# Down operands of a feed-forward loaded three units ahead, and a sample fold done by transposes

## The chip, the core and the metric

One core of a Trainium2 chip runs the whole kernel in one launch. The metric is the device time of that launch in microseconds (us); lower is better. A core has TensorE (in the profile PE for its matmuls and PEld for its weight loads), VectorE (DVE), ScalarE (ACT), GpSimd (POOL) and SyncE (SP), which here issues the DMAs. Each engine runs its own queue in order.

## The reference

One layer of a hybrid decoder on 2048 prompt tokens and 64 sample tokens of width 1024. The two sub-layers are a mixer (sliding-window attention beside gated linear attention) and a feed-forward network. The change lies in the second, whose core is:

```python
h = rms_norm(x, g_ffn_pre)
u = jax.nn.relu(jnp.einsum('btd,df->btf', h, w_up))      # w_up (1024, 4096)
f = jnp.einsum('btf,fd->btd', u * u, w_down)             # w_down (4096, 1024)
x = x + rms_norm(f, g_ffn_post)
```

All of it is in float32, for prompt and sample alike.

## The kernel before

Float32 precision is made of three passes: each operand is split into a rounded high part (a ScalarE copy) and the rest (a VectorE subtraction), and a product is high x high, high x low and low x high (`three`, `split_copy`). For the prompt the feed-forward uses a scheme with seven products in place of eight for a 2x2 blocking, so there are sums of blocks before and after the products.

The prompt tokens are worked in two halves (`sb` 0 and 1). For each half `up(sb, fc, ...)` runs over 16 strips of 256 hidden features: seven products of 12 matmuls in the order `UP_ORDER`, with sums and squares behind each (`taken`), and at the end a store of the strip's seven operand blocks to the DRAM tensor `s_d` (1792 KB). Numbers 0, 8 and 9 in the order are the sample tokens, in the first half only: 0 and 8 are their product with the strip's weights, into the bank `sam` (rows are token parts high and low, 128 of them), and `both` is its copy in SBUF. Step 9 turns it to features x tokens and adds the high and low rows, with a matmul against the constant `fold` (two identities on top of one another). `sample_features` squares, splits and stores the result to `sm_d`.

`down(sb)` then walks 112 units: seven products `p` in `DOWN_ORDER`, each over the 16 strips. A unit needs an operand `s` (from `s_d`) and an operand `t` (from `w_down`, or from sums of its blocks kept in `t_d`). `down_operand` loads each into a raw tile (tag `r`, the profile's `rs` and `rt`) and splits it into `o0` and `o1`. Unit n multiplies four 128-column slices, 12 matmuls of 128x512, into the banks `dn`. The next unit's operands are fetched at the head of a unit. The raw tiles have two buffers (three for `s` in the second half), the split ones three. For p in 1, 2, 3 and 5 of the first half two more matmuls take the sample tokens (`dsam`), whose features lie in two tiles `smp` of 512 KB, loaded by `load_sample`.

Beside the units runs a list of work, `todo`, of which some goes out behind each unit: `gather` adds banks into the result rows, `finish` loads the residual rows (`x1`, in the profile `fx`), normalizes and stores a result, `load_h` splits the second half's inputs that `fetch_h` loaded at the units in `H_FETCH`. `prepare_last` and `finish_last` do the last four row tiles. `gains_post` loads the gains of the last norm (`gfpost`).

The order on an engine is set in two ways. Calls through `te`, `ac` and `dv` (class `InOrder`) keep the program's order among themselves. Everything else, the DMAs on SyncE among it, is placed by a scheduler at compile time: it takes what is ready, in the order of the program where several are. A tile of a pool with `bufs=n` can be written again when its reader n tiles back is done. `tc.issue_after(ins)` asks for what is traced within it to be queued behind `ins`.

Of the kernel before, what the change touches and what calls it, by code (L numbers as in the profile page):

```python
# [115 lines left out]
def f32(ap):  # L116
    return ap.bitcast(F32)
# [23 lines left out]
def hybrid_step_kernel(ctx: ExitStack, tc: tile.TileContext, I, O):  # L141
# [1447 lines left out]
    def squared(t, src=None):  # L1589
        ac.activation(t, t if src is None else src, AF.Relu)  # L1590
        ac.activation(t, t, AF.Square)

    def up(sb, fc, before, steps=iter(())):
# [28 lines left out]
        def taken(p):  # L1622

            if p == 1:
                ac.activation(s(1), X, AF.Copy)
            elif p == 5:
                ac.activation(s(3), Z, AF.Copy)
            elif p == 7:
                add(3, s(3), V)
            elif p == 6:  # L1630
                add(1, s(1), Y)
                add(3, s(3), s(1))
                squared(s(3))
# [12 lines left out]

# [121 lines left out]
    def sample_features(fc, sam):  # L1768
        sq = U["sam"].tile([P, 2, NS], F32, tag="samq", name=f"samq_{fc}", bufs=1)
        parts = U["sam"].tile([P, 2, 2 * NS], F32R, tag="samp", name=f"samp_{fc}", bufs=1)  # L1770
        squared(sq, sam[:, FC : FC + 2 * NS].rearrange("p (u t) -> p u t", u=2))
        split_by(ac, dv, parts[:, :, :NS], parts[:, :, NS:], sq)
        nc.sync.dma_start(sm_d[:, fc], f32(parts))

    def down_operand(sb, p, fc, which):

        name, kind = f"{'st'[which]}_{sb}_{p}_{fc}", "st"[which]
        raw = Dp[kind + "r"].tile([P, BT], F32, tag="r", name=f"r{name}", bufs=3 if (sb, which) == (1, 0) else 2)
        hi, lo = (Dp[kind + "s"].tile([P, BT], F32R, tag=f"o{u}", name=f"o{u}{name}", bufs=3) for u in range(2))
# [7 lines left out]
        nc.sync.dma_start(raw, src)  # L1787
        split_copy(hi, lo, raw)
        return hi, lo

# [15 lines left out]
    def finish(i, fi):  # L1806

        n = rows(i)
        x1 = Dp["x1"].tile([P, D], F32, tag="x1", name=f"fx1_{i}", bufs=1)
        nc.sync.dma_start(x1[:n], x1_d[i])  # L1810
# [9 lines left out]
        nc.sync.dma_start(y_rows(i), fi[:n])  # L1820
        yield 1.3
# [3 lines left out]
    def prepare_last(i, j, fi):  # L1825

        x1 = Dp["lx"].tile([P, D], F32, tag=f"lx{j}", name=f"lx1_{i}", bufs=1)
        nc.sync.dma_start(x1, x1_d[i])
# [19 lines left out]
    smp = {}  # L1848

    def load_sample(u, part):  # L1850

        n = NFC // 2
        smp[part] = Dp["smp"].tile([P, n, 2 * NS], F32R, tag=f"smp{part}", name=f"smp_{u}_{part}", bufs=1)
        nc.sync.dma_start(f32(smp[part]), sm_d[:, part * n : (part + 1) * n, u])

    def gather(sb, p, j, f, p_):

# [60 lines left out]
    def down(sb):  # L1918
# [1 line left out]


        units = [(p, fc) for p in DOWN_ORDER for fc in range(NFC)]
        parts, f, todo, late = {}, {}, deque(), DOWN_ORDER[-1]
        fetched, loaded = (dict(zip(units_, H_ORDER)) for units_ in (H_FETCH, [(p, fc + 4) for p, fc in H_FETCH]))

        def fetch(n):
            if n < len(units) and n not in parts:
                parts[n] = [down_operand(sb, *units[n], which) for which in range(2)]

        def products(n, j):  # L1930
            p, fc = units[n]
# [1 line left out]
            q = slice(j * P, (j + 1) * P)  # L1933
            return three(banks[j], sh[:, q], sl[:, q], th, tl, fc == 0, fc == NFC - 1, te)

        fetch(0)
        for n, (p, fc) in enumerate(units):
            if fc == 0:
                banks = [down_bank(f"dn_{sb}_{p}_{j}") for j in range(4)]
# [14 lines left out]
            if (sb, p, fc) == (0, late, 0):  # L1954
# [3 lines left out]
                weights = ahead_of_up()  # L1958
                next(weights)
                todo.extend((*waiting, weights))  # L1960
            fetch(n + 1)
            for j in range(4):
                done = products(n, j)
            if sam is not None:
                for u, t in enumerate(parts[n][1]):
                    te.matmul(
                        sam, smp[fc // 8][:, fc % 8], t, start=fc + u == 0, stop=fc == NFC - 1 and u == 1
                    )
# [38 lines left out]
    fold = cpool.tile([P, NS], F32, name="fold")  # L2007
    nc.vector.tensor_tensor(fold, ident[:, :NS], ident[:, NS:], op=ALU.add)
    last_rows = residual(*early.pop(0), te, ac, dv)
    sums_13(0, 0, dv)  # L2010
    run(load_h(0, 5, ac, dv))
# [76 lines left out]
```

## Time and profile before

| what | value |
|---|---|
| median of 3 runs | 2264.04 us (2259.86 to 2265.18) |
| the profiled execution | 2263.19 us |
| its span, first to last instruction | 2261.4 us |
| mean granted TensorE clock | 0.995 |
| strips of `up`, first half | about 940 to 1283 us |
| units of `down`, first half | 1283 to 1633 us |
| units of `down`, second half | 1941 us to the end |

In a timeline row stand the start, the busy time, the engine, the line of the code, the operation, what is written and read with its shape, how many were merged, and in brackets how long the engine was idle before and who ended that. In a list of waits the three numbers are the total in us, the count and the longest. In a row of the windows stand the busy times of PE, PEld, DVE, ACT and POOL with their counts, then the granted clock, the DMA engines' busy share and GB/s. Matmuls overlap: the time from start to start counts, not the busy time of one.

### The profile page before, as it was taken

To read this page: it belongs to the slowest core of one execution; us is meant where nothing else is said; L and a number is where in the kernel's file an instruction comes from. 1 tells how busy PE (TensorE), PEld (TensorE's weight loads), DVE (VectorE), ACT (ScalarE), POOL (GpSimd) and SP (SyncE) were. 2 spreads that over 40 slices of the span, in tenths; PEclk is the share of its full clock that TensorE was granted. 3 is DMA by queue.
4 is the path that set the end of the run, shared out by engine and by line. 5 is a ranking of instruction groups with operands and counts; after the bars stand their busy time and mean duration, and the time that the engine had idled before them with its cause. 6 is when DMAs were issued, how large, how long until landed. Compare 5 with 4: busy or idle time off the path is not lost.

```text
span 2261.4 us, 34140 instructions
## 1 busy us (share of the span) xinstructions
PE 2183.5 (97%) x11816; PEld 1868.7 (83%) x11816; DVE 1529.9 (68%) x3102; ACT 1221.4 (54%) x2594; POOL 259.4 (11%) x417
## 2 busy tenths in 40 slices
PE   8999999999999999999999999999999999999998
PEld 7888888999998887788888788887888888788876
DVE  5888877776765565777788664447676666455566
ACT  5778766556664444555545564334544454454444
POOL 3566422111111110000000000000000000000000
PEclk9999999999999999999999999999999999999999
DMA  6334322214335558967777885557644443766675
GB/s 231 119 133 143 102 90 82 67 57 148 126 122 196 184 181 312 313 222 243 251 254 253 284 290 181 180 167 231 195 179 154 154 154 140 252 201 198 192 241 169
DMA packets 237256, 417.81 MB, mean 185 GB/s; under 512 B 25172, under 2 KB 137276, under 8 KB 232972
## 3 DMA queue, kind: packets, MB, share of 16 engines
q1 hardware_dynamic: 237084, 415.64, 54.8%
q8 instruction: 93, 1.52, 0.3%
q14 instruction: 79, 0.65, 0.1%
HBM read 268.44 MB, written 148.18 MB: 184 GB/s over the span
## 4 chain that ended last, share of the span: by engine, by line
PE 64%; DVE 15%; ACT 8%; DMA 8%; issue 3%; POOL 1%; SPq 0%; DVEq 0%; ACTq 0%; POOLq 0%
PE dn L130 21%; PE uc L130 6%; PE ua L130 6%; PE out L1250 6%; PE gproj L130 5%; PE ud L130 3%; PE ue L130 3%; PE ub L130 3%; DMA rt<-t_d 3%; DVE s L130 2%; PE proj L130 2%; PE dsam L130 1%; DVE pl L130 1%; PE o L130 1%; PE sam L130 1%
## 5 line engine op out<-in xcount | busy, mean ns | idle before, releaser
L130 PE MATMUL dn<-o0t,o0s 128*128 128x512 f32 x896 | 350.7, 391 | 9.0 <-ACT o0t L218 8.8
L130 PE MATMUL dn<-o1t,o0s 128*128 128x512 f32 x896 | 351.3, 392 | 3.1 <-DVE o1t L219 3.1
L130 PE MATMUL dn<-o0t,o1s 128*128 128x512 f32 x896 | 349.9, 391 | 0.0
L219 DVE TENSOR_TENSOR o1s<-rs,o0s 128x512 fp32r<-128x512 f32 x224 | 154.6, 691 | 197.2 <-ACT o0s L218 182.8
L218 ACT ACTIVATE o0s<-rs 128x512 fp32r<-128x512 f32 x224 | 141.1, 630 | 249.9 <-PE dn L130 206.0
L130 PE MATMUL gproj<-wg,gx 128*128 128x384 f32 x1408 | 268.5, 343 | 0.1
L130 PEld LDWEIGHTS gproj<-wg,gx 128*128 128x128 f32 x1408 | 241.6, 189 | 4.5 <-issue 4.3
L130 ACT ACTIVATE st<-st 128x512 f32<-128x512 f32 x224 | 141.1, 630 | 158.9 <-DVE st L130 154.9
L130 PEld LDWEIGHTS dn<-o0t,o0s 128*128 128x128 f32 x896 | 168.6, 188 | 48.9 <-ACT o0t L218 11.9
L130 PEld LDWEIGHTS dn<-o1t,o0s 128*128 128x128 f32 x896 | 168.5, 188 | 43.7 <-DVE o1t L219 7.9
L130 PEld LDWEIGHTS dn<-o0t,o1s 128*128 128x128 f32 x896 | 168.5, 188 | 35.0
L219 DVE TENSOR_TENSOR o1t<-rt,o0t 128x512 fp32r<-128x512 f32 x224 | 153.9, 687 | 64.3 <-ACT o0t L218 63.9
L218 ACT ACTIVATE o0t<-rt 128x512 fp32r<-128x512 f32 x224 | 139.6, 624 | 91.7 <-DMA rt<-t_d 70.0
L130 PE MATMUL uc<-H,s 128*128 128x512 f32 x768 | 186.7, 391 | 0.0
L130 PE MATMUL ua<-H,w 128*128 128x512 f32 x744 | 179.2, 390 | 0.0
L130 PEld LDWEIGHTS uc<-H,s 128*128 128x128 f32 x768 | 144.1, 188 | 31.9
L130 PEld LDWEIGHTS ua<-H,w 128*128 128x128 f32 x744 | 138.7, 188 | 28.2
L1250 PE MATMUL out<-wo,mt 128*128 128x512 f32 x680 | 158.9, 392 | 1.9 <-ACT mt L218 1.8
L1250 PEld LDWEIGHTS out<-wo,mt 128*128 128x128 f32 x680 | 126.5, 188 | 28.6 <-ACT mt L218 2.1
L208 POOL TENSOR_TENSOR frs<-rs_v,half 128x1 f32<-128x1 f32 (+1 forms) x13 | 8.4, 657 | 1230.2 <-DVE rs_v L206 1230.2
L130 DVE TENSOR_TENSOR st<-st 128x512 f32<-128x512 f32 x160 | 110.7, 692 | 35.1 <-ACT st L130 31.8
L130 ACT ACTIVATE s<-t 128x1024 fp32r<-128x1024 f32 x62 | 65.8, 1061 | 93.5 <-PE ud L130 29.0
(388 smaller groups left out, 4231.2 us busy)
## 6 DMA issues: line engine op xcount, KB each, us to landing
s_d<-st SPq DMA_DIRECT2D x32, 1792.0 KB, 7.6
rs<-s_d SPq DMA_DIRECT2D x224, 256.0 KB, 2.9
raw<-in_w_up SPq DMA_DIRECT2D x64, 512.0 KB, 5.2
rt<-t_d SPq DMA_DIRECT2D x128, 256.0 KB, 3.3
rt<-in_w_down SPq DMA_DIRECT2D x96, 256.0 KB, 2.8
t<-in_w_down SPq DMA_DIRECT2D x64, 256.0 KB, 3.7
t_d<-t SPq DMA_DIRECT2D x32, 512.0 KB, 6.6
gx<-xt_d SPq DMA_DIRECT2D x28, 512.0 KB, 4.8
```

What stands on the lines that cost most here:

```text
L130: ins = call(*a, **k)
L208: nc.gpsimd.tensor_tensor(out, v[:n], e, op=ALU.pow)
L218: nc.scalar.activation(hi, src, AF.Copy)
L219: vector.tensor_tensor(lo, src, f32(hi), op=ALU.subtract)
L1250: te.matmul(banks[c], x, w[:, c * 512 : (c + 1) * 512], start=k + u == 0, stop=k == KT - 1 and u == len(products) - 1,)
```

## The change

- `UP_ORDER`: the sample's second product (8) comes before product 3 in place of behind it.
- Step 9 is two transposes of 128x128 through the identity. `sample_features` adds the two halves itself, with a ScalarE copy and a VectorE add, before the squares.
- `down_operand` is cut in two: `down_raw` loads, three units ahead, into three raw buffers (four in the second half); the split is called two units ahead.
- The sample features are loaded by unit, 64 KB each, into four buffers (`load_sample`).
- `H_FETCH` is moved: its first fetch goes from unit (6, 0) to (6, 6), the one at (6, 8) goes, and one at (3, 8) comes. The gains are called behind unit 26 in place of 8. The loads of `x1` stand in an issue-after clause on the latest unit's last matmul.

```diff
-UP_ORDER, UP_FIRST = (1, 5, 7, 0, 6, 3, 8, 2, 9, 4), (1, 0, 2, 8, 5, 7, 9, 6, 3, 4)
+UP_ORDER, UP_FIRST = (1, 5, 7, 0, 6, 8, 3, 2, 9, 4), (1, 0, 2, 8, 5, 7, 9, 6, 3, 4)
-H_FETCH = ((6, 0), (6, 8), (1, 0), (1, 8), (5, 0), (5, 8), (3, 0))
+H_FETCH = ((6, 6), (1, 0), (1, 8), (5, 0), (5, 8), (3, 0), (3, 8))
...
                 for u in range(2):
-                    te.matmul(
-                        sam[:, FC + u * NS : FC + (u + 1) * NS], both[0][:, u * P : (u + 1) * P], fold, start=True, stop=True
-                    )
+                    te.transpose(sam[:, FC + u * P : FC + (u + 1) * P], both[0][:, u * P : (u + 1) * P], ident)
...
-        squared(sq, sam[:, FC : FC + 2 * NS].rearrange("p (u t) -> p u t", u=2))
+        turned = sam[:, FC:].rearrange("p (u a t) -> p u a t", u=2, a=2)
+        ac.activation(sq, turned[:, :, 1], AF.Copy)
+        dv.tensor_tensor(sq, sq, turned[:, :, 0], op=ALU.add)
+        squared(sq)
...
-    def down_operand(sb, p, fc, which):
+    def down_raw(sb, p, fc, which):
...
-        raw = Dp[kind + "r"].tile([P, BT], F32, tag="r", name=f"r{name}", bufs=3 if (sb, which) == (1, 0) else 2)
-        hi, lo = (Dp[kind + "s"].tile([P, BT], F32R, tag=f"o{u}", name=f"o{u}{name}", bufs=3) for u in range(2))
+        raw = Dp[kind + "r"].tile([P, BT], F32, tag="r", name=f"r{name}", bufs=4 if sb else 3)
...
         nc.sync.dma_start(raw, src)
+        return raw
+
+    def down_operand(sb, p, fc, which, raw):
+
+        name, kind = f"{'st'[which]}_{sb}_{p}_{fc}", "st"[which]
+        hi, lo = (Dp[kind + "s"].tile([P, BT], F32R, tag=f"o{u}", name=f"o{u}{name}", bufs=3) for u in range(2))
         split_copy(hi, lo, raw)
...
-        nc.sync.dma_start(x1[:n], x1_d[i])
+        with tc.issue_after(latest[0].ins):
+            nc.sync.dma_start(x1[:n], x1_d[i])
...
-    def load_sample(u, part):
-
-        n = NFC // 2
-        smp[part] = Dp["smp"].tile([P, n, 2 * NS], F32R, tag=f"smp{part}", name=f"smp_{u}_{part}", bufs=1)
-        nc.sync.dma_start(f32(smp[part]), sm_d[:, part * n : (part + 1) * n, u])
+    def load_sample(p, fc):
+
+        t = Dp["smp"].tile([P, 2 * NS], F32R, tag="smp", name=f"smp_{p}_{fc}", bufs=4)
+        nc.sync.dma_start(f32(t), sm_d[:, fc, int(p in (2, 3))])
+        return t
...
+        def load(n):
+            if n < len(units) and n not in raws_:
+                raws_[n] = [down_raw(sb, *units[n], which) for which in range(2)]
+                if sb == 0 and units[n][0] in (1, 2, 3, 5):
+                    smp[n] = load_sample(*units[n])
+
         def fetch(n):
             if n < len(units) and n not in parts:
-                parts[n] = [down_operand(sb, *units[n], which) for which in range(2)]
+                load(n)
+                parts[n] = [down_operand(sb, *units[n], which, raws_[n][which]) for which in range(2)]
...
+        for n in range(3):
+            load(n)
         fetch(0)
+        fetch(1)
...
-            fetch(n + 1)
+            load(n + 3)
+            fetch(n + 2)
             for j in range(4):
                 done = products(n, j)
+            latest[:] = [done]
...
-            if n == 8:
+            if n == 26:
                 with tc.issue_after(done.ins):
-                    for part in range(2 * (sb == 0)):
-                        load_sample(0, part)
                     gains_post(sb)
-            if p == 5 and sb == 0 and fc in (8, NFC - 1):
-                load_sample(1, fc // 9)
```

More of the change, by code (lines that the diff above doesn't have):

```diff
@@ L1827, in prepare_last @@
         x1 = Dp["lx"].tile([P, D], F32, tag=f"lx{j}", name=f"lx1_{i}", bufs=1)
-        nc.sync.dma_start(x1, x1_d[i])
+        with tc.issue_after(latest[0].ins):
+            nc.sync.dma_start(x1, x1_d[i])
         ssq = Dp["n"].tile([P, 4], F32, tag="lssq", name=f"lssq_{i}", bufs=4)
@@ L1846, in finish_last @@
             nc.sync.dma_start(y_rows(i)[:, dd], fg[:, dd])
[L1848 to L1854 removed]
+    latest = []
+    def load_sample(p, fc):
+        t = Dp["smp"].tile([P, 2 * NS], F32R, tag="smp", name=f"smp_{p}_{fc}", bufs=4)
+        nc.sync.dma_start(f32(t), sm_d[:, fc, int(p in (2, 3))])
+        return t
     def gather(sb, p, j, f, p_):
@@ L1922, in down @@
         units = [(p, fc) for p in DOWN_ORDER for fc in range(NFC)]
-        parts, f, todo, late = {}, {}, deque(), DOWN_ORDER[-1]
+        parts, raws_, smp, f, todo, late = {}, {}, {}, {}, deque(), DOWN_ORDER[-1]
         fetched, loaded = (dict(zip(units_, H_ORDER)) for units_ in (H_FETCH, [(p, fc + 4) for p, fc in H_FETCH]))
+        def load(n):
[3 more added lines that the diff above has]
+                    smp[n] = load_sample(*units[n])
         def fetch(n):
             if n < len(units) and n not in parts:
-                parts[n] = [down_operand(sb, *units[n], which) for which in range(2)]
+                load(n)
+                parts[n] = [down_operand(sb, *units[n], which, raws_[n][which]) for which in range(2)]
         def products(n, j):
@@ L1966, in down @@
                     te.matmul(
-                        sam, smp[fc // 8][:, fc % 8], t, start=fc + u == 0, stop=fc == NFC - 1 and u == 1
+                        sam, smp[n], t, start=fc + u == 0, stop=fc == NFC - 1 and u == 1
                     )
             del parts[n]
-            if n == 8:
+            if n == 26:
                 with tc.issue_after(done.ins):
-                    for part in range(2 * (sb == 0)):
-                        load_sample(0, part)
                     gains_post(sb)
-            if p == 5 and sb == 0 and fc in (8, NFC - 1):
-                load_sample(1, fc // 9)
             if sb == 0 and (p, fc) in loaded:
@@ L2006, in hybrid_step_kernel @@
     down_halves = ((fc, half) for fc in range(NFC) for half in range(2))
-    fold = cpool.tile([P, NS], F32, name="fold")
-    nc.vector.tensor_tensor(fold, ident[:, :NS], ident[:, NS:], op=ALU.add)
     last_rows = residual(*early.pop(0), te, ac, dv)
```

## The prediction

> **What bounds the kernel now.** I read the page's head first, then the list of waits for the whole span, then the same list for single stretches, and last the timelines around the waits.
>
> ```profile
> span 2261.4 us, 34140 instructions
> PE 2183.5 (97%) x11816; PEld 1868.7 (83%) x11816; DVE 1529.9 (68%) x3102; ACT 1221.4 (54%) x2594; POOL 259.4 (11%) x417
> ...
> s_d<-st SPq DMA_DIRECT2D x32, 1792.0 KB, 7.6
> rs<-s_d SPq DMA_DIRECT2D x224, 256.0 KB, 2.9
> ```
>
> TensorE is busy for 97% of the span, and the change leaves the number of down products as it is. So only TensorE's own holes and its few small instructions can be won. The list of waits of TensorE names the holes that the change can reach (columns: total us, times, longest):
>
> ```profile
> PE dn L130 <- ACT o0t L218: 8.8, 7, 3.4
> PE sam L130 <- ACT both L130: 3.2, 4, 1.4
> PE dn L130 <- DVE o1t L219: 3.1, 9, 1.3
> ```
>
> The same list over three stretches: 1545 to 1645 (first two rows), 1950 to 2050 (next two), 2050 to the end (last two):
>
> ```profile
> PE dn L130 <- ACT o0t L218: 2.7, 3, 1.4
> PE dn L130 <- DVE o1t L219: 2.0, 4, 1.3
> ...
> PE dn L130 <- ACT o0t L218: 1.5, 1, 1.5
> PE dn L130 <- DVE o1t L219: 0.4, 2, 0.2
> ...
> PE dn L130 <- ACT o0t L218: 1.1, 2, 0.9
> PE dn L130 <- DVE o1t L219: 0.7, 3, 0.2
> ```
>
> These, with one hole of 3.4 us at 1297, are nearly all the waits of the down products. What a hole costs beyond its idle time is in TensorE's timeline:
>
> ```profile
> 1293.73 0.39 PE L130 MATMUL dn<-o1t,o0s 128*128 128x512 f32 x1
> ...
> 1296.68 0.39 PE L130 MATMUL dn<-o0t,o1s 128*128 128x512 f32 x1
> 1300.44 0.80 PE L130 MATMUL dn<-o0t,o0s 128*128 128x512 f32 x1 [3.37 <-ACT o0t L218]
> ...
> 1303.90 0.40 PE L130 MATMUL dn<-o1t,o0s 128*128 128x512 f32 x1
> ```
>
> From 1293.73 to 1296.68 lie 13 steps, so one product takes 0.227 us from start to start, and a unit of 12 takes 2.72 us. From 1296.68 to 1303.90 lie 8 steps, which took 7.22 us in place of 1.82: this hole cost 5.4 us, of which some 1.9 are the slow products behind it. The windows show the granted clock dip there, and a second stretch with as many products missing at full clock:
>
> ```profile
> 1280.00:1340.00 60.00, 56.41 (x241) 45.31 (x240) 36.09 (x51) 34.49 (x55) 0.00 (x0) 0.97 0.89 292
> 1460.00:1520.00 60.00, 60.00 (x263) 49.09 (x262) 26.43 (x43) 21.57 (x38) 0.00 (x0) 1.00 0.51 166
> 1520.00:1580.00 60.00, 55.98 (x240) 44.37 (x238) 40.59 (x59) 28.22 (x48) 3.35 (x5) 1.00 0.70 227
> ```
>
> The Trainium skill, page "TensorE: Matmul & The Clock Gate", section "What's actually happening", says that one wholly idle window of about 3.4 us puts the array on half its clock; the 3.37 us of idleness and the clock of 0.97 agree, and by that rule a hole that is only shortened already loses its slow products.
>
> **Why the operands were late.** SyncE's queue and ScalarE around the hole at 1297:
>
> ```profile
> 1283.29 0.43 SPq L1854 DMA_DIRECT2D smp<-sm_d  x1
> ...
> 1288.79 0.42 SPq L200 DMA_DIRECT2D gfpost<-in_g_ffn_post  x1
> 1291.07 0.32 SPq L1710 DMA_DIRECT2D s_d<-st  x1
> 1291.43 0.43 SPq L1787 DMA_DIRECT2D rs<-s_d  x1
> ...
> 1299.24 0.63 ACT L218 ACTIVATE o0s<-rs 128x512 fp32r<-128x512 f32 x1 [7.76 <-DMA rs<-s_d]
> ```
>
> The 1.8 MB store of the last strip went out just ahead of the operand load for unit 5, with half-megabyte loads of samples and gains ahead of both, so a load that takes 2.9 us in the median took nearly 8. Two raw buffers let the load of unit n+2 start only when unit n is split. The rows also show that the place in the program does not set the place in the queue. The gains stand in the code behind the products of unit 8, under an issue-after clause on a matmul; they were issued at 1288.79, while unit 5 began at 1300.44. Loads go out as soon as a buffer is free.
>
> **Part by part.**
>
> *Fold by transposes.* TensorE's timeline at the last fold, and at a run of eight transposes of the same 128x128 shape:
>
> ```profile
> 1279.90 0.55 PE L130 MATMUL sam<-fold,both 128*128 128x64 f32 x4
> 1280.26 3.00 PE L130 MATMUL ue<-H,w 128*128 128x512 f32 x12
> ...
> 761.12 1.06 PE L1436 MATMUL xnT<-ident,x 128*128 128x128 f32 x8 [1.10 <-DVE x L1426]
> 761.93 2.33 PE L1250 MATMUL out<-wo,mt 128*128 128x512 f32 x9
> ```
>
> A fold takes 0.36 us of TensorE, eight transposes 0.81, so two take 0.20. Over 16 strips that is 16 x 0.16 = 2.6 us. Between 0 (transposes as dear as the fold) and 2.6 I take 2.6, the measured shape.
>
> *Sample product moved ahead of product 3.* The copy `both` gets a further product (12 steps, 2.72 us) before TensorE asks for it. The longest of its waits is 1.4 us, so all 3.2 us go. The first strip keeps its own order, so a few tenths could stay.
>
> *More work behind the fold.* Each strip gains one ScalarE copy and one VectorE add, and ScalarE must then wait for that add:
>
> ```profile
> 1020.76 0.26 ACT L130 ACTIVATE samq<-sam 128x128 f32<-128x128 f32 x1
> ...
> 1022.57 1.07 ACT L130 ACTIVATE w<-raw 128x1024 fp32r<-128x1024 f32 x1 [0.86 <-PE ue L130]
> ...
> 1028.25 0.60 ACT L130 ACTIVATE st<-uc 128x512 f32<-128x512 f32 x1 [2.13 <-PE uc L130]
> ...
> 1020.89 2.15 DVE L130 TENSOR_TENSOR st<-st 128x512 f32<-128x512 f32 x3 [0.88 <-ACT st L130]
> 1022.95 0.29 DVE L130 TENSOR_TENSOR samp<-samq,samp 128x128 fp32r<-128x128 f32 x1
> ```
>
> The add comes behind VectorE's three, at 1022.95. ScalarE's three remaining sample steps (0.31 each, one size above the 0.26) then end near 1024.2, so the split queued behind them starts 1.6 us late. ScalarE idles 2.13 us before 1028.25, which takes that up before TensorE asks for anything: that split feeds a product four products later. I take 0; uncovered it is 1.6 per strip.
>
> *Raw operands three units ahead, three buffers (four in the second half).* At 1297, one more buffer lets the load of unit 5 go out when unit 2 is split, before the store at 1291.07. The whole 5.4 us go; unit 7, behind the store, still has two units in hand. In the stretch from 1557 another thing holds SyncE:
>
> ```profile
> 1557.90 0.34 SPq L1820 DMA_DIRECT2D out_y_prompt<-f  x1
> 1558.29 0.42 SPq L1810 DMA_DIRECT2D fx<-x_d  x1
> 1559.69 0.32 SPq L1787 DMA_DIRECT2D rs<-s_d  x1
> ...
> 1561.50 0.32 SPq L1787 DMA_DIRECT2D rt<-t_d  x1
> 1565.02 0.34 SPq L1820 DMA_DIRECT2D out_y_prompt<-f  x1
> ```
>
> Each result store stands at the head of the queue until its add is done; two units of loads go out per cycle of 7.1 us, where TensorE wants two per 5.4. A deeper buffer does not mend the cycle, it lends one unit once: of the 4.7 us of waits (2.7 + 2.0) I take 2.72. Bounds: 0, and 23 missing products x 0.227 = 5.2. In the second half the waits are 1.9 (1.5 + 0.4) and 1.8 (1.1 + 0.7), each far below the lead won; I take all 3.7.
>
> *Splits two units ahead in the program.* Still three split buffers, so TensorE frees them as before. 0; the gathers queued behind them get no later than the products they wait for.
>
> *Fetches moved.* The seven H fetches (two loads each on SyncE, with two ScalarE copies of the 1.07 shape and two VectorE subtractions) and the gains (one load) go to later units, the x loads get an issue-after clause on a matmul. As the gains' row shows, none of this need move them in the queue; 0, covered by ScalarE and VectorE, which are busy 21.57 and 26.43 of 60 us in the quiet stretch. Four sample loads of 512 KB become 64 small ones, one SyncE issue of 0.43 each, at most, in 64 units of 14 x 0.227 = 3.18 us; the half megabyte at 1283.29 leaves the crowded start. 0 on the path.
>
> Sum: 2.6 + 3.2 + 5.4 + 2.7 + 3.7 = 17.6. The profiled execution took 2263.19 us (span 2261.4), the median of the runs is 0.85 above it. 2263.2 - 17.6 + 0.85 = 2246.4 us.
>
> **Rivals.**
>
> *The DMA engines are the limit, not the lead.* For it: their busy share of 0.89 at 292 GB/s in 1280 to 1340; loads asked for earlier would merely queue earlier. Against it: 0.51 and 0.70 elsewhere. Only the fold's 5.8 stay: 2258.2, within the bound of 0.3% (6.8 us), which is about what a measurement can tell here.
>
> *The edits of place do nothing.* The gains' row speaks for that; it is in my sum at 0 and changes no number.
>
> *ScalarE's new wait reaches TensorE, slower.* At the end of each strip the in-order chain of ScalarE stands still behind VectorE's add. It decides if TensorE needs something behind that split within the strip. Price 16 x 1.6 = 25.6: 2246.4 + 25.6 = 2272.0. Against it speak the 2.13 us of idleness.
>
> *The small sample loads hold the operand loads, slower.* A sample buffer is freed only by TensorE; a load waiting for it blocks SyncE. If no unit stayed in hand, a unit would take a landing and two ScalarE copies, 2.9 + 2 x 0.63 = 4.2 against 3.18: 64 x 1.0, 2310. It needs both the three units of lead and the four buffers to be gone. The Trainium skill, page "DMA: Bandwidth & Descriptors", section "Rules for kernel authors", says to coalesce many small transfers into large ones, and these are 64 KB each where the old ones are 512; no run here yet shows such a load.
>
> **How the numbers follow.** Forecast 0.75, DMA limit 0.13, ScalarE's wait 0.08, sample loads 0.04. So faster by over 0.3% 0.75, within 0.13, slower 0.12. The low end takes the 1557 stretch at 5.2 instead of 2.7 (2243.9) and the 4 us by which the fastest run lies under the median: 2240. The high end reaches to the DMA case at 2258.2: 2259.
>
> **What would show it.** Right: no wait of `sam` for `both`; two matmul records per strip for the turn where the fold has four; no hole of TensorE near 1297 and a clock of 1.00 there; ScalarE's waits for raw operands gone at the start of both down stages; some waits left after the first results of the first half. Wrong: the same holes with the loads issued earlier but landing no sooner (DMA limit), new waits of `ua` or `ub` for ScalarE's splits, or SyncE waiting for TensorE at the sample loads with ScalarE waiting for operands behind it.

## The result and the profile after

The changed kernel takes 2241.72 us (median of four runs, 2239.81 to 2243.32), the kernel before 2262.93 (four runs, 2259.86 to 2265.18). The ratio is 0.991 with a 95% interval of 0.9898 to 0.9921: 21.2 us faster, where 17.6 were forecast (2246.4). The time lies within the forecast range, near its low end. Three of the five terms that lead to it were off: most of one was lost to a wait that the forecast had at nothing, and two came out larger.

The head of the page of after, and TensorE's waits in the whole span for `dn` and `sam` (total us, times, longest):

```profile
span 2239.4 us, 34249 instructions
PE 2173.6 (97%) x11784; PEld 1865.2 (83%) x11784; DVE 1531.7 (68%) x3117; ACT 1217.7 (54%) x2610; POOL 261.3 (12%) x417
...
PE dn L130 <- DVE samq L130: 2.0, 1, 2.0
PE dn L130 <- DVE o1t L219: 0.7, 3, 0.3
PE dn L130 <- ACT o0t L218: 0.6, 1, 0.6
PE sam L130 <- ACT both L130: 0.5, 1, 0.5
```

The waits for operand splits fell from 11.9 us in 16 places to 1.3 in four, the one for `both` from 3.2 to 0.5. One wait is new: `dn` for `samq`, 2.0 us, once.

Why the operands are now in time is seen best from ScalarE. Its waits in 1275 to 1345, before (first two rows) and after (next three), and in 1945 to 2000, before (one row) and after (one):

```profile
ACT o0s L218 <- DMA rs<-s_d: 11.4, 5, 7.8
ACT o0t L218 <- DMA rt<-t_d: 6.9, 7, 2.1
...
ACT o0s L218 <- PE dn L130: 14.2, 11, 1.7
ACT H L1495 <- DMA hraw<-h_d: 14.1, 7, 3.0
ACT o0t L218 <- DMA rt<-t_d: 0.2, 1, 0.2
...
ACT o0t L218 <- DMA rt<-t_d: 22.6, 11, 5.2
...
ACT o0s L218 <- PE dn L130: 29.2, 19, 1.6
```

Before, the splits waited for loads. After, they wait for TensorE to free a split buffer, which is how a pipeline looks that is far enough ahead. One wait for loads grew, that of the copies of H: 14.1 us, where before had 6.4. It matters below. The operand loads themselves became no quicker: the page gives these medians from issue to landing (last column, us), where before had 7.6 and 2.9:

```profile
s_d<-st SPq DMA_DIRECT2D x32, 1792.0 KB, 8.7
rs<-s_d SPq DMA_DIRECT2D x224, 256.0 KB, 3.5
```

To place the gain I split both spans at the starts of TensorE's stages, taken from its timeline: the up stage, then the seven down products of each half (192 `dn` matmuls each; one without a hole and without the sample products that products 2 to 5 of the first half carry takes 43.5 us). Products are counted by their place in `DOWN_ORDER`: product 6 is the one numbered 7, which some of the expectations below call the seventh product. The up stage is counted from its first sample product, 2.9 us behind its first product. All in us:

| stage | before | after | gain |
|---|---|---|---|
| ahead of the feed-forward | 928.84 | 926.68 | 2.17 |
| up stage of the first half | 354.25 | 347.60 | 6.65 |
| down, first half, product 1 | 49.24 | 47.35 | 1.89 |
| products 2 to 5 | 206.64 | 207.06 | -0.42 |
| product 6 | 50.28 | 44.94 | 5.34 |
| up stage of the second half | 307.79 | 307.79 | 0.00 |
| down, second half, product 1 | 46.53 | 43.52 | 3.01 |
| product 6 | 46.60 | 43.52 | 3.08 |
| the rest (products 7, products 2 to 5 of the second half, the end) | 271.23 | 270.96 | 0.27 |

The first row belongs to no edit: in the executions that follow, this part ends anywhere between 926.0 and 931.5 us. So a single span carries some 2.5 us either way, and below I read the stages first.

### The profile page after: what moved, and what is told of

The parts are those of the page before. It is cut to its first block, busy times and chain, and to the rows that moved or that the text cites. A ratio compares the mean times of both kernels' runs of the same rounds, so it can differ in the third digit from the quotient of the medians.

```text
span 2239.4 us, 34249 instructions
## 1 busy us (share of the span) xinstructions
PE 2173.6 (97%) x11784; PEld 1865.2 (83%) x11784; DVE 1531.7 (68%) x3117; ACT 1217.7 (54%) x2610; POOL 261.3 (12%) x417
## 4 chain that ended last, share of the span: by engine, by line
PE 73%; DVE 13%; ACT 7%; DMA 4%; issue 2%; POOL 1%; SPq 0%; DVEq 0%; ACTq 0%; POOLq 0%
PE dn L130 26%; PE ua L130 7%; PE uc L130 7%; PE gproj L130 6%; PE out L1250 6%; PE ud L130 4%; PE ue L130 4%; PE ub L130 4%; DVE s L130 2%; PE proj L130 2%; PE dsam L130 1%; PE sam L130 1%; DVE pl L130 1%; PE o L130 1%; DMA rt<-t_d 1%
```

## The new hole, and the one that shrank

TensorE at the start of the first half's down stage in after, with the matching rows of ScalarE and VectorE:

```profile
1275.42 0.39 PE L130 MATMUL dn<-o0t,o1s 128*128 128x512 f32 x1
1277.78 0.68 PE L130 MATMUL dn<-o0t,o0s 128*128 128x512 f32 x1 [1.97 <-DVE samq L130]
1278.26 0.63 PE L130 MATMUL dn<-o1t,o0s 128*128 128x512 f32 x1
...
1281.25 0.41 PE L130 MATMUL dn<-o0t,o1s 128*128 128x512 f32 x1
1281.50 0.40 PE L130 MATMUL dn<-o0t,o0s 128*128 128x512 f32 x1
...
1274.12 0.26 ACT L130 ACTIVATE samq<-sam 128x128 f32<-128x128 f32 x1
...
1277.67 0.65 ACT L130 ACTIVATE samq<-samq 128x128 f32<-128x128 f32 x2 [1.72 <-DVE samq L130]
...
1274.34 0.68 DVE L130 TENSOR_TENSOR st<-st 128x512 f32<-128x512 f32 x1
...
1276.15 0.69 DVE L219 TENSOR_TENSOR o1s<-rs,o0s 128x512 fp32r<-128x512 f32 x1
1276.75 0.69 DVE L130 TENSOR_TENSOR st<-st 128x512 f32<-128x512 f32 x1
1277.36 0.28 DVE L130 TENSOR_TENSOR samq<-samq,sam 128x128 f32<-128x128 f32 x1
```

The third bank that the first down unit takes is one of the two `b`, which the last strip's `sam` still holds. ScalarE has copied its half by 1274.4, but the new add of the other half stands in VectorE's queue from then until 1277.36, behind adds of `st` and splits of the first operands. TensorE finds its bank closed for that long. The step from 1275.42 to 1277.78 is 2.36 us in place of 0.23, and the next eight products start 0.43 to 0.48 apart in place of 0.227: together 3.8 us. In the up stage the same add is as late on every strip, and nothing there needs the bank soon:

```profile
L130 PE MATMUL sam<-ident,both x32: 272/273/328, 938.3 to 1271.4; 128*128 128x128 f32 x32
...
  ACT samq L130: 43.1, 16
```

(the group of the transposes, and who waited for `samq`: us, times). ScalarE waits 2.7 us per strip for the add, 43.1 in all, and TensorE not once within the strips. The first row also shows the two records per strip that were expected. What they cost TensorE is in its timeline of the last strip:

```profile
1271.31 0.38 PE L130 MATMUL sam<-ident,both 128*128 128x128 f32 x2
1271.44 0.94 PE L130 MATMUL ue<-H,w 128*128 128x512 f32 x3
```

From the two transposes to the next product it is 0.13 us (0.14 in most strips), where the fold took 0.36.

The windows that the prediction quoted, and SyncE around them, in after:

```profile
1280.00:1340.00 60.00, 59.70 (x259) 48.71 (x258) 34.40 (x48) 33.09 (x53) 0.00 (x0) 0.99 0.86 284
1520.00:1580.00 60.00, 59.09 (x258) 47.93 (x257) 45.44 (x67) 31.31 (x53) 4.94 (x5) 1.00 0.79 248
...
1281.59 0.32 SPq L1787 DMA_DIRECT2D rs<-s_d  x1
...
1283.30 0.32 SPq L1708 DMA_DIRECT2D s_d<-st  x1
...
1312.06 0.42 SPq L200 DMA_DIRECT2D gfpost<-in_g_ffn_post  x1
...
1555.88 0.34 SPq L1827 DMA_DIRECT2D out_y_prompt<-f  x1
...
1562.84 0.34 SPq L1827 DMA_DIRECT2D out_y_prompt<-f  x1
```

TensorE runs 259 and 258 products where it ran 241 and 240, with the DMA share about as high as before (0.86 for 0.89) or higher (0.79 for 0.70). The down stage begins 8.8 us earlier in after (1274.28 for 1283.09), so the stretches do not lie quite alike, but the hole of the first window lay well inside it. (That of the second did not: a further wait of 1.43 us ended at 1580.42, just outside.) The 0.99 of the first window is the end of the slow products of the new hole. In the stage the store `s_d` leaves no earlier than before, 9.0 us behind its first product (8.0 before), but the load at 1281.59 ahead of it is the seventh of its kind, that of unit 6, where only five stood ahead of the store before. Around the results of the first product the stores still follow each other at 7 us (1555.88, 1562.84): the cycle did not change, yet most of its holes went (product 6 still takes 1.4 us more than one without a hole). The loads of `x1`, which got the issue-after clause, stand right behind the stores as before (1556.31 after, 1558.29 before), so the clause moved nothing here; no run takes it out alone.

## Experiments

All ratios are against the kernel before, run on the same chip beside them, with 95% intervals. The columns up, p1, p6, q1, q6 are the stages of the table above from the profiled execution (p and q are the down products of the first and the second half). Each is a single execution. Beside the four kernels from fold_only to shallow the kernel before had a median of 2261.18, beside banks, fold_back, turned_late and fetch_back 2260.17, beside the last four 2259.04; so kernels of different groups are compared by their ratios.

| kernel | median us | ratio | up | p1 | p6 | q1 | q6 |
|---|---|---|---|---|---|---|---|
| before | 2262.93 | 1 | 354.25 | 49.24 | 50.28 | 46.53 | 46.60 |
| after | 2241.72 | 0.9910 (0.9898 to 0.9921) | 347.60 | 47.35 | 44.94 | 43.52 | 43.52 |
| fold_only | 2252.97 | 0.9962 (0.9947 to 0.9977) | 347.64 | 50.12 | 48.84 | 44.89 | 46.11 |
| lead_small | 2242.56 | 0.9914 (0.9900 to 0.9929) | 353.27 | 43.53 | 45.10 | 43.81 | 43.52 |
| moves_only | 2259.69 | 0.9984 (0.9973 to 0.9995) | 353.24 | 47.73 | 52.14 | 45.18 | 45.50 |
| shallow | 2255.28 | 0.9970 (0.9960 to 0.9980) | 347.76 | 51.01 | 46.56 | 46.83 | 48.56 |
| banks | 2238.16 | 0.9902 (0.9888 to 0.9915) | 347.93 | 43.56 | 44.76 | 43.56 | 43.52 |
| fold_back | 2244.87 | 0.9934 (0.9922 to 0.9947) | 350.52 | 46.43 | 44.37 | 43.53 | 43.52 |
| turned_late | 2246.53 | 0.9937 (0.9924 to 0.9949) | 349.89 | 47.70 | 44.88 | 43.59 | 43.52 |
| fetch_back | 2242.53 | 0.9919 (0.9906 to 0.9933) | 348.03 | 47.93 | 44.98 | 43.52 | 43.52 |
| split_near | 2243.65 | 0.9924 (0.9907 to 0.9941) | 347.85 | 49.74 | 46.26 | 43.95 | 43.84 |
| store_pool | 2266.28 | 1.0026 (1.0012 to 1.0040) | 353.37 | 50.67 | 50.13 | 46.37 | 46.94 |
| banks_pool | 2247.51 | 0.9943 (0.9923 to 0.9962) | 347.92 | 43.97 | 46.46 | 43.67 | 45.37 |
| lead_order | 2241.71 | 0.9914 (0.9899 to 0.9930) | 350.38 | 43.92 | 44.61 | 44.03 | 43.52 |

### The parts alone

**fold_only**: before, with the transposes and the moved sample product, and nothing else of the change.

```diff
-UP_ORDER, UP_FIRST = (1, 5, 7, 0, 6, 3, 8, 2, 9, 4), (1, 0, 2, 8, 5, 7, 9, 6, 3, 4)
+UP_ORDER, UP_FIRST = (1, 5, 7, 0, 6, 8, 3, 2, 9, 4), (1, 0, 2, 8, 5, 7, 9, 6, 3, 4)
...
-                    te.matmul(
-                        sam[:, FC + u * NS : FC + (u + 1) * NS], both[0][:, u * P : (u + 1) * P], fold, start=True, stop=True
-                    )
+                    te.transpose(sam[:, FC + u * P : FC + (u + 1) * P], both[0][:, u * P : (u + 1) * P], ident)
...
-        squared(sq, sam[:, FC : FC + 2 * NS].rearrange("p (u t) -> p u t", u=2))
+        turned = sam[:, FC:].rearrange("p (u a t) -> p u a t", u=2, a=2)
+        ac.activation(sq, turned[:, :, 1], AF.Copy)
+        dv.tensor_tensor(sq, sq, turned[:, :, 0], op=ALU.add)
+        squared(sq)
```

> The kernel before with the sample fold by transposes and the new place of product 8 alone. Theory (leads): the strips of the first half gain the 6.6 us that the changed kernel's trace shows between the first sample product and the first down product, and the first unit then waits for the bank that the new VectorE add still reads (2.0 us of idleness in the changed kernel, with slow products behind it 3.8). The hole near the sixth unit and those of the later stages stay as before, since nothing is loaded earlier: 2256 to 2262 in all, 2259 the middle. Rival (fold): the fold is most of the gain of 21 us, by freeing VectorE and ScalarE in the strips: under 2252.

The up stage fell by 6.6 us, and the wait for the bank came with the add, lead or no lead:

```profile
PE dn L130 <- DVE samq L130: 2.3, 1, 2.3
...
1277.88 0.47 PE L130 MATMUL dn<-o0t,o0s 128*128 128x512 f32 x1 [2.33 <-DVE samq L130]
1278.19 0.40 PE L130 MATMUL dn<-o1t,o0s 128*128 128x512 f32 x1
```

At 2252.97 it is faster than I had expected, because holes of the shallow pipeline, which this kernel keeps, came out smaller in it (product 6 by 1.4, the first of the second half by 1.6, and near the sixth unit a hole that cost 2.2 us where before had 5.4). The sizes of those holes differ from build to build by that much; the experiments on them are read with this in mind.

**lead_small**: the loads three units ahead, the splits two ahead, the deeper buffers and the small sample loads, with the old fold, order and fetches. (The clause on the `x1` loads stays. The small sample loads belong to it for their room: two tiles of 512 KB become four of 64 KB, and the deeper raw buffers take 512 KB more in the first half.)

```diff
-UP_ORDER, UP_FIRST = (1, 5, 7, 0, 6, 8, 3, 2, 9, 4), (1, 0, 2, 8, 5, 7, 9, 6, 3, 4)
+UP_ORDER, UP_FIRST = (1, 5, 7, 0, 6, 3, 8, 2, 9, 4), (1, 0, 2, 8, 5, 7, 9, 6, 3, 4)
...
-H_FETCH = ((6, 6), (1, 0), (1, 8), (5, 0), (5, 8), (3, 0), (3, 8))
+H_FETCH = ((6, 0), (6, 8), (1, 0), (1, 8), (5, 0), (5, 8), (3, 0))
...
-            if n == 26:
+            if n == 8:
```

(against after; the fold as in before)

> The kernel before with the lead alone: raw operands three units ahead in three or four buffers, splits two ahead, and the small sample loads, without which the buffers have no room in SBUF; the fold, the places of the H fetches and of the gains are those of before. Theory (leads): the holes of the later stages go (5.4 in the first half at the seventh product, 3.0 and 3.1 in the second half) and the one near the sixth unit (5.4): 2263 - 16.9 = 2246, range 2244 to 2250. Rival (places): the H fetches and gains, still in the queue at the head of the first half, keep the hole near the sixth unit open: about 2251; if they carry the later stages too, 2256 or more.

It is as fast as the whole change: 2242.56, below the range that I expected. The holes of the down stages went, that at the head of the first half included (43.53); 1.6 us are left in product 6. The DMA engines are as loaded as ever (0.89 in 1280 to 1340, 0.79 in 1520 to 1580). So the lead is what the down stages gain from, the DMA engines are not their limit, and what the whole change wins in the up stage it gives back in part in the bank.

**moves_only**: before, with the moved fetches and the small sample loads.

```diff
-H_FETCH = ((6, 0), (6, 8), (1, 0), (1, 8), (5, 0), (5, 8), (3, 0))
+H_FETCH = ((6, 6), (1, 0), (1, 8), (5, 0), (5, 8), (3, 0), (3, 8))
...
-            if n == 8:
+            if n == 26:
```

(the sample loads as in the change)

> The kernel before with only the fetches moved: H fetches and gains at the units of the changed kernel, sample features loaded by unit in 64 KB; two raw buffers (three for s in the second half) and one unit of lead as before, and the fold as before. Theory (leads): places do little, 2260 to 2264, with the hole near the sixth unit there still, perhaps smaller as 2 MB fewer stand in the queue before it. Rival (places): the hole near the sixth unit goes, 2263 - 5.4 = 2257.5 or less; the holes of the seventh product and of the second half stay in both, since no fetch that was moved goes out there, except the gains at the head of the second half (3.0).

2259.69, and by the ratio a gain of 1 to 6 us. Its executions scatter: three of ten took 2253 to 2255 us, the others 2259 to 2264, and the profiled one 2262.30. In that one the hole near the sixth unit shrank a little (product 1 47.73) and product 6 grew (52.14). Both lie within what builds of the shallow pipeline differ by, so a small gain is shown and its place is not.

### The change with one part undone

**shallow**: two raw buffers again, with the loads still asked for three units ahead in the program.

```diff
-        raw = Dp[kind + "r"].tile([P, BT], F32, tag="r", name=f"r{name}", bufs=4 if sb else 3)
+        raw = Dp[kind + "r"].tile([P, BT], F32, tag="r", name=f"r{name}", bufs=3 if (sb, which) == (1, 0) else 2)
```

> The changed kernel with the raw buffers of before (two; three for s in the second half), the loads still called three units ahead. Theory (leads): it is the buffers and not the place of the call that give the lead, so the holes of the seventh product (5.4) and of the second half (3.0 and 3.1) come back: 2241.7 + 11.5 = 2253, and up to 2257 if the hole near the sixth unit comes back too. Rival (places): the calls and moved fetches are enough, 2241 to 2244.

The holes of the second half are back (46.83 and 48.56), and the ratio is that of the fold alone. There it is the buffers that carry the lead, not the place of the load in the program. The wait for the bank grew, and more slow products stand behind it:

```profile
1281.46 0.77 PE L130 MATMUL dn<-o0t,o0s 128*128 128x512 f32 x1 [3.15 <-DVE samq L130]
1282.03 0.63 PE L130 MATMUL dn<-o1t,o0s 128*128 128x512 f32 x1
...
1287.54 0.40 PE L130 MATMUL dn<-o0t,o1s 128*128 128x512 f32 x1
```

That wait and its slow products cost 6.2 us (9.62 us from 1277.92, the start of the product before, to 1287.54, for 15 steps of 0.227), and they are why product 1 takes 51.01. The hole near the sixth unit did not come back with two raw buffers: the longest other step in product 1 is 0.74 us. Six `rs` loads, those of units 0 to 5, stand ahead of the store here, where five did before.

**fetch_back**: the H fetches and the gains back in their old units.

```diff
-H_FETCH = ((6, 6), (1, 0), (1, 8), (5, 0), (5, 8), (3, 0), (3, 8))
+H_FETCH = ((6, 0), (6, 8), (1, 0), (1, 8), (5, 0), (5, 8), (3, 0))
...
-            if n == 26:
+            if n == 8:
```

> The changed kernel with the H fetches and the gains at the units of before (first at the head of the half, gains behind unit 8). Theory (leads): nothing comes back, 2240.5 to 2243. Rival (places): half a megabyte of gains and the H loads stand again before the operand loads at the head of the halves and a hole opens near the sixth unit: 2244 or more.

2242.53, the five stages of the table within 0.6 us of after. Beside the lead the moved fetches are worth nothing; if anything they cost 0.8 us in product 2 of the first half (52.14 in after, 51.38 here).

**turned_late**: transposes, but the sample product behind product 3 as before.

```diff
-UP_ORDER, UP_FIRST = (1, 5, 7, 0, 6, 8, 3, 2, 9, 4), (1, 0, 2, 8, 5, 7, 9, 6, 3, 4)
+UP_ORDER, UP_FIRST = (1, 5, 7, 0, 6, 3, 8, 2, 9, 4), (1, 0, 2, 8, 5, 7, 9, 6, 3, 4)
```

> The changed kernel with product 8 behind product 3 again. Theory of the prediction: TensorE waits for the copy of the sample product once more, up to 3.2 us over the strips: 2243 to 2245. Rival: with VectorE and ScalarE otherwise placed the copy is in time anyway, 2241 to 2242.5.

```profile
PE sam L130 <- ACT both L130: 3.2, 2, 2.9
```

The wait for `both` is back at 3.2 us in total, though in two places where before had four, and the up stage is 2.3 longer. At 2246.53 the kernel is slower than I expected; product 2 of the first half took 1.2 more (53.38) and the part ahead of the feed-forward 2.5, and why product 2 did stays open.

**fold_back**: the new order and lead, with the fold as a matmul.

```diff
-                    te.transpose(sam[:, FC + u * P : FC + (u + 1) * P], both[0][:, u * P : (u + 1) * P], ident)
+                    te.matmul(
+                        sam[:, FC + u * NS : FC + (u + 1) * NS], both[0][:, u * P : (u + 1) * P], fold, start=True, stop=True
+                    )
```

(and without the copy and the add behind it)

> The changed kernel with the fold by matmul again (no ScalarE copy, no VectorE add behind it), the new place of product 8 kept. Theory (bank): the hole at the head of the first half goes, since the bank is read by one ScalarE step alone, -3.8; the folds cost 16 x 0.16 = 2.6 more: 2240.5, so the transposes on the whole cost a little. Rival (fold): the transposes are what they gain, 2.6, and no more: 2244.3.

I expected 2240.5 and measured 2244.87. The wait for the bank is gone, as it should be without the add, but three other holes came in product 1 (46.43) and more in product 2 (53.52). ScalarE around the second of them:

```profile
1313.97 0.62 ACT L218 ACTIVATE o0t<-rt 128x512 fp32r<-128x512 f32 x1
1318.78 1.06 ACT L1495 ACTIVATE H<-hraw 128x1024 fp32r<-128x1024 f32 x1 [4.19 <-DMA hraw<-h_d]
1319.74 0.61 ACT L218 ACTIVATE o0s<-rs 128x512 fp32r<-128x512 f32 x1
```

A copy of H stands in ScalarE's queue and waits 4.2 us for its load, and the split that TensorE needs next stands behind it. Either the matmul fold or the later units of the H fetches could have brought that about; the next kernel takes them apart:

**lead_order**: fold_back with the H fetches and the gains in their old units too.

```diff
-H_FETCH = ((6, 6), (1, 0), (1, 8), (5, 0), (5, 8), (3, 0), (3, 8))
+H_FETCH = ((6, 0), (6, 8), (1, 0), (1, 8), (5, 0), (5, 8), (3, 0))
...
-            if n == 26:
+            if n == 8:
```

> The kernel lead_small with product 8 ahead of product 3: the lead, the new order and the small sample loads, with the fold by matmul and the fetches where they were. Theory (copies): the holes in the kernel fold_back behind its 14th unit came of the moved H fetches, whose ScalarE copies wait for their loads with operand splits behind them; with the fetches of before the first product of the first half takes 43.5 us, and the waits for the copy of the sample product (2.5 us) go: 2240. Rival: the holes come with the fold by matmul, 46.4 for that stage and 2243.

2241.71, and no hole at the head (43.92). All waits of TensorE from 1270 on in it:

```profile
PE dn L130 <- DVE o1t L219: 0.8, 4, 0.2
PE dsam L130 <- ACT fs L1898: 0.3, 1, 0.3
```

So the holes need the moved H fetches. They do not come with these every time: after has the moved fetches too, ScalarE waits for H there as well (14.1 us), and its product 1 has no hole for a split. Without the transposes and the moved fetches the kernel is as fast as with the whole change.

**split_near**: the splits one unit ahead in the program, as before, and the loads three ahead.

```diff
-        fetch(1)
...
-            fetch(n + 2)
+            fetch(n + 1)
```

> The changed kernel with the splits called one unit ahead as before; the loads stay three ahead in three or four buffers. Stage read: the sixth product of the first half, 50.3 us before, 44.9 in the changed kernel, 43.7 without any hole. Theory (two covers): the prediction lent that stage one unit (2.72 us) and 5.35 came, since the split called two units ahead is a second unit of cover; without it the stage takes about 47.5, and the kernel 2244.5. Rival (buffers): the third raw buffer is all, the stage stays at 44.6 to 45.2 and the kernel at 2241 to 2243.

Product 6 took 46.26, between the two expectations. Beside shallow (46.56) and the two kernels themselves this reads: before 50.28, either cover alone (deeper buffers, or loads and splits called earlier) 46.3 to 46.6, both 44.9. Each alone brings 3.7 to 4.0 of the 5.3 us, give or take what builds of the shallow pipeline differ by (48.84 to 52.14 in the four that have neither cover). The same holds for the hole near the sixth unit, which is absent here and in shallow; the 49.74 of product 1 is the wait for the bank once more (2.87 us, with slow products). In the second half the buffers alone do nearly all (43.95 and 43.84).

### The bank, and the stores

**banks**: the whole change, with the down products taking their banks in another order, so that the first unit takes `a`, `c`, `c`, `d` and no `b`.

```diff
-        return bank([P, 512], "aabbccd"[turn[0] % 7], name)
+        return bank([P, 512], "aaccdbb"[turn[0] % 7], name)
```

> The changed kernel with the down banks taken in the order aaccdbb in place of aabbccd, so that the first product of a half writes a, c, c, d and the bank of the last strip's sample product comes a product later. Theory (bank): the hole of 2.0 us behind the first two blocks of the first unit is TensorE waiting for the VectorE add that reads that bank; with another bank it goes, and the nine slow products behind it: from the first to the second product of the first half 47.4 - 3.8 = 43.6 us, 2241.7 - 3.8 = 2238 in all. Rival (queue): the operands or their splits are not ready there either, so the hole stays under another name: 2241 to 2243.

```profile
1276.19 0.39 PE L130 MATMUL dn<-o0t,o1s 128*128 128x512 f32 x1
1276.41 0.39 PE L130 MATMUL dn<-o0t,o0s 128*128 128x512 f32 x1
```

These are the sixth and the seventh product of the stage, which in after lay 2.36 us apart. Product 1 took 43.56 us, 3.8 less than in after, the price read from the hole. Its median, 2238.16, is the lowest of all kernels here; it was taken beside a lower median of before, and the interval of its ratio overlaps that of the change, so what is shown is the 3.8 us of the stage.

**store_pool**: before, with the stores of the results issued by GpSimd, to see whether a store at the head of SyncE's queue is what paces the cycle of 7.1 us.

```diff
-        nc.sync.dma_start(y_rows(i), fi[:n])
+        nc.gpsimd.dma_start(y_rows(i), fi[:n])
```

> The kernel before with the stores of finished results (13 of them, the last four row tiles excepted) issued by GpSimd in place of SyncE. Theory (head of the queue): the stores that wait for their add keep the operand loads behind them from being issued; without them the sixth product of the first half falls from 50.3 to about 45 us, that of the second half from 46.6 to about 44, and the kernel from 2261 to about 2253. Rival (DMA engines): the transfers themselves are too many there, the stages stay within 0.7 us of before, and so does the kernel.

Product 6 stayed at 50.13, and product 7 grew from 43.73 to 47.18; the kernel is slower than before, which neither expectation had. Waits of SyncE's queue (two rows) and of GpSimd in 1550 to 1600:

```profile
SPq L1787 <- DVE o1s L219: 12.0, 13, 2.0
SPq L1787 <- DVE o1t L219: 11.7, 15, 2.7
...
POOL out_y_prompt L1820 <- DVE f L1798: 13.8, 3, 7.4
```

With the stores gone from it, SyncE waits for the split of the raw buffer that it wants to fill. So the store at the head is not the only thing that spaces the loads; with two raw buffers the splits space them as well. It isn't a clean test, since the stores now held GpSimd's queue for up to 7.4 us, with the norms' work behind them. What alone would pace this cycle stays open.

**banks_pool**: banks with the same stores on GpSimd.

```diff
-        nc.sync.dma_start(y_rows(i), fi[:n])
+        nc.gpsimd.dma_start(y_rows(i), fi[:n])
```

> The kernel banks with the same 13 stores issued by GpSimd. Theory (head of the queue): the 1.1 us that the sixth product of the first half still loses go, 2238.2 - 1.1 = 2237. Rival (DMA engines): no change, 2237.5 to 2239; or slower where an issue by GpSimd costs its queue, which the norms of the results pass through.

2247.51, 9 us above banks by median and by ratio, of which 7.3 lie in four stages: the first half's product 6 (46.46) and product 7 (45.41 for 43.29), the second half's up stage (309.46 for 307.79) and product 6 (45.37). Stores that wait for another engine cost more in GpSimd's queue than in SyncE's, with lead and without.

## Why the prediction was right, point by point, and where it was not

**Up stage.** Forecast 2.6 + 3.2 = 5.8. Four executions with the old fold and order (before, lead_small, moves_only, store_pool) have a mean of 353.5 us, the two with only the order changed (fold_back, lead_order) 350.45, those with both (after, fold_only, shallow, banks, fetch_back, split_near, banks_pool) 347.8: 3.1 for the order, 2.6 for the transposes. The sum was right; the 6.65 of the two profiles holds 0.7 by which that execution of before lay above its like. That each term came out as forecast is in part luck. Two transposes take 0.14 us and not 0.20, which is 0.22 per strip and 3.3 us in all (the transposes of after against the folds of lead_order, over the 16 strips), and with both edits some wait for `both` stays (0.4 to 2.2 us in the seven, none in lead_order and 0.6 in fold_back), where the forecast had it all gone. Taken the other way round, the transposes alone (turned_late, 349.89) bring 3.6 and the order on top of them 2.1.

**Head of the first half.** Forecast 5.4, net 1.9. The hole near the sixth unit went as forecast: two more loads ahead of the store, and unit 7, behind it, with units in hand (its load went out at 1284.91, its split at 1291.68 waited for TensorE and not for the load, and the unit begins at 1297.15). The reason given, one more buffer, is enough (split_near) but not needed: in shallow the load of unit 5 goes ahead of the store with two raw buffers, where only the calls of loads and splits come earlier than in moves_only, the fold and the `x1` clause apart. The forecast took earlier splits at 0. What failed is the step "More work behind the fold", taken at 0. I followed the late ScalarE chain to the products that need it, and did not ask which PSUM bank the new add still reads and who takes that bank next. The add's lateness cost nothing in the strips, as said, and 3.8 us once, where the stage ends. The price varies with the slow products behind it: 2.5 us in fold_only, which has none, and 6.2 in shallow. banks shows it by taking another bank, fold_back, lead_order and lead_small by having no such add.

**The stretch from 1557.** Forecast 2.72, measured 5.34. The step "it lends one unit once" was the mis-sized term, together with "Splits two units ahead" at 0: the earlier calls are a second cover, and split_near and shallow show each cover bringing most of it alone. (Shallow does not part the splits two ahead from the loads three ahead.) The bound of 5.2 was too low as well, since the window it was read from ends at 1580, within the stretch: product 6 of before is 6.8 us longer than one without a hole. The cycle of the result stores stayed at 7 us as I had said; that the store at its head paces the loads was only argued, and store_pool speaks against it as the only cause; what paces them stays open.

**Second half.** Forecast 3.7, measured 6.1 (3.0 + 3.1). The holes went as forecast. The term was too small because it counted the idle times of the list of waits; what a hole costs is the stage's length over 43.5, 3.0 and 3.1 in before. The list counts idleness from the end of the product before, 0.39 us after its start, where the next would have started after 0.227, so each of the eight waits costs some 0.16 more than it shows; the steps just behind a hole are longer too.

**Fetches moved.** At 0, right by fetch_back. The reason was too strong: "the place in the program does not set the place in the queue". The gains left at 1312.06 in place of 1288.79, and in fold_back the later H copies did hold ScalarE.

**The rivals.** DMA limit: lead_small and the second half refute it, with the `rs` loads landing later (3.9 us in lead_small and 3.5 in after, for 2.9) and no hole. ScalarE's wait per strip: it came, longer than priced (2.7 us for 1.6, 16 times), and ScalarE's idleness took it up. Small sample loads: this group of after shows all 64 (issue in ns, least, median, most; first and last start), and the second row SyncE's waits at them in 1279 to 1530:

```profile
L1861 SPq DMA_DIRECT2D smp<-sm_d x64: 319/320/466, 1279.4 to 1516.0; - x64
...
SPq L1861 <- PE dsam L130: 67.8, 52, 1.6
```

So half of this rival came true: SyncE does stand at the sample loads until TensorE frees a buffer, 67.8 us in 52 waits, with operand loads queued behind. The other half did not: the longest wait is 1.6 us, and in 1322 to 1530 ScalarE waited for an operand's load once, 0.7 us, and TensorE never for a sample load. The three units of lead took it up. The seven whose landing is on record landed 1.9 us after their issue in the median. The Trainium skill, page "DMA: Bandwidth & Descriptors", section "Rules for kernel authors", advises against such splitting; here it cost nothing that shows on the path, and it frees 768 KB, where the deeper raw buffers of the first half take 512.

That the sum came within 3.6 us of the measured gain is in part luck, since the errors had opposite signs: 3.5 too much at the head, 2.6 and 2.4 too little in the other two, and 0.9 in the up stage; what is left (1.2) is no more than the medians move.

## What to carry to other kernels

When a change gives a stage's last step a further reader, ask which buffer or PSUM bank that reader holds, where it stands in its engine's queue, and which instruction of the next stage takes the bank; a rotation that begins elsewhere can make it free. To size a hole, compare the length of the stretch with that of one without a hole, and don't add up idle times. Lead lies in buffers first, and calling loads and splits earlier in the program can be a second cover but did not replace the buffers in the second half. Where the lead is there, the order of other fetches hardly matters, except that a copy which waits for its load holds all that is queued behind it.

## What the runs showed of the hardware that was not expected

The granted clock fell to half after far less idleness than 3.4 us, and not always. After 1.97 us of idleness (after, 1277.78) it was half for 3.4 us, and products take 0.63 us in place of 0.39; in the row of that window the granted clock is the 0.50:

```profile
1277.87:1281.28 3.41, 3.41 (x9) 2.64 (x10) 1.67 (x4) 1.80 (x6) 0.00 (x0) 0.50 0.93 334
```

After 3.15 us (shallow, 1281.46) fourteen products were slow, for about twice as long. After 2.33 us (fold_only, 1277.88) none was. One place is the same in all the kernels: near 710 us TensorE idles 2.13 to 2.16 us, and slow products follow it in three of the 14 traces (before, fetch_back, store_pool). So the length of the idleness alone does not decide.

The prediction had drawn on the Trainium skill, page "TensorE: Matmul & The Clock Gate", section "What's actually happening", for one idle window of about 3.4 us as what halves the clock, and had worked out that a hole which is only shortened loses its slow products. The measurement decides: 1.97 us sufficed, so a shortened hole can keep them, and already the 3.37 us of before are less than the 3.41 us that were slow behind them. The same section of the Trainium skill gives the window a length of 3413 ns, and the slow stretches of 3.4 us and of about twice that agree with it. What decides between none, one and two such lengths was not tried.
